# Moving weight splits, odd-key and rotated-query remainders and the token shift of a two-block decoder from ScalarE and VectorE to GpSimd

## The chip, the cores and the metric

One core of one Trainium2 chip runs the whole program. The metric is the device time of one execution in microseconds; the kernel before was timed in three runs. All profile times are from one profiled execution of it.

## What is computed

Two decoder blocks follow each other on 512 tokens of width 1024. The first has a gated unit, a sparse attention, cross-attention to a memory and a feed-forward part. The second has two layers, and the change is about these. In each layer one wide projection of the normed tokens (and of 256 context tokens) feeds three branches: a window attention "a", an attention "b" whose keys, values and queries are projected from small latents, and a gated convolution "c". The branches are gated and merged:

```python
def rms_norm_2(x, g):
    xf = x.astype(jnp.float32)
    y = xf * lax.rsqrt(jnp.mean(xf * xf, axis=-1, keepdims=True) + EPS)
    return (y * g.astype(jnp.float32)).astype(x.dtype)
...
    q = (rms_norm_2(q_lat, g_qa) @ w_qb).reshape(B, T, H_B, NOPE_B + ROPE_B)
    kv = (rms_norm_2(kv_lat, g_kva) @ w_kvb).reshape(B, T, H_B, NOPE_B + V_B)
...
    m = (jax.nn.sigmoid(ga) * ((ya * jax.nn.silu(za)) @ w_branch[0])
         + jax.nn.sigmoid(gb) * ((yb * jax.nn.silu(zb)) @ w_branch[1])
         + jax.nn.sigmoid(gc) * ((yc * jax.nn.silu(zc)) @ w_branch[2]))
    return m @ w_o
```

## The kernel before

Every operand of a matmul is held as a rounded high half and a remainder, the low half, and each product is three matmuls (`mm3`, lines 415 to 418: high by high, low by high, high by low). So all weights are **split** after they are loaded. The class `Stream` (lines 183 to 329) does it: SP loads chunks into tiles `raw`; `stat` (line 224) lets ScalarE sum squares for a scale; `total` (lines 425 to 433) turns the sums into the scale, by way of a VectorE sum, a matmul with ones, a VectorE step (L431), a power on GpSimd (L432) and a reciprocal on VectorE (L433); `pump` (line 237 on) writes the high half `wh` and, at the next call, `finish` (line 285 on) the low half `wl`. A ring of 9 pairs of `wh` and `wl` is filled ahead of use. Weights marked `fr` stay in 32 bits (high by ScalarE L266, low by VectorE L267); the others become 16-bit (high by ScalarE L273, or by GpSimd L271 where the block is marked `pool=True`; low by VectorE L291, in pieces of 512 columns).

The order of the work is written as Python generators: `tick` advances a clock of estimated costs, and calls the weight stream, the delayed chains (such as `norm_chain`) and the background attention. A scheduler then sets the order of each engine's queue by a priority that follows program order and by its own estimate of when each instruction is ready. Each engine takes its queue strictly in order.

In each layer, after the projections of branch a and the convolution, come the **latent stages**: latents kl and ql are projected and normed (`ev_kl`, `ev_ql`), and then `attention(b_items(...))` goes over 8 heads with 4 or 5 query tiles each. An item is: the S matmuls (L416 to L418, tile `S`, two buffers), the maximum on VectorE (L705), the exponential on ScalarE (L721, tile `P`), transposes on TensorE (L734), their high part on ScalarE (L738) and low part on VectorE (L739), and the output matmuls (L755). Between the items stand projections: `qb_head` makes the rotated queries of the next head (VectorE L1861, ScalarE L1862, VectorE L1863 for the latent tokens), `kb_pair` and `kb_odd` the keys (odd heads by way of a staging tile `kst`, split on ScalarE and VectorE at L421 and L422), `ev_vb` the values, and `agate` the gate of branch a with the weights `za`. The weights of the heads are split by `sp_` in `qb_blk` (3 or 4 moves each, ScalarE L1911 and VectorE L1912) and by the `fr` path for `kb_blk` and `vb_blk`. The merge's first gate and branch weights are read ahead while the attention still runs.

At a **layer boundary** `res_chain` (line 2179 on) adds the output to the tokens, and `norm_chain` (line 611 on) makes the next layer's normed tokens: squares on ScalarE (L614), `rstd` on GpSimd (six instructions, L404 to L412), gain on VectorE (L618), shift on VectorE (L620), then transposes on TensorE (L630). The boundaries lie near 815 to 845 us (first block to layer 0, four token tiles) and near 1705 to 1765 us (layer 0 to layer 1, six tiles, called 4, 5, 0, 1, 2, 3 in the order of their work). Two context tiles near 664 us take the same path.

## Time and profile before

| what | value |
|---|---|
| time, median of 3 runs (lowest, highest) | 2424.09 us (2421.36, 2431.43) |
| the profiled execution's own time | 2421.47 us |
| its span, first to last instruction | 2419.7 us |
| mean granted TensorE clock | 0.978 of full speed |
| attention b of layer 0 | about 1140 to 1340 us |
| attention b of layer 1 | about 2000 to 2140 us |

Times in rows are microseconds from the span's start unless marked ns. PE is TensorE, DVE VectorE, ACT ScalarE, POOL GpSimd. In a group's row the number behind the shape is the count, then busy time and mean ns of one, then the engine's idle time just before these instructions and what ended it. Square brackets in a timeline row hold the same idle time.

### The profile page before, as it was taken

Reading aid. Unit: us, or ns where it says so; the run is one execution under the profiler, and the core shown is the slowest. Engines: PE = TensorE matmul, PEld = TensorE weight load, DVE = VectorE, ACT = ScalarE, POOL = GpSimd, SP = SyncE. Lnnn points to the kernel's source line nnn. Section 1 sums busy time; section 2 is a strip of 40 time slices with the busy share of each in tenths; the row PEclk is TensorE's granted clock in tenths of the full one; section 3 lists DMA queues with packets and bytes.
Section 4 is the critical chain, followed back from the end, with each engine's and each line's share of the span. In section 5 each row is a group of like instructions: output and inputs, shape, how many; then the busy total and the mean of one; then the engine's idle time right before and its main releaser. Section 6 shows DMA issues by size and latency. Waiting matters only on the chain. (4 is left out here: it accounts for less than half of the span.)

```text
span 2419.7 us, 38066 instructions
## 1 busy us (share of the span) xinstructions
PE 2261.3 (93%) x14342; PEld 1505.2 (62%) x14342; DVE 1544.2 (64%) x3136; ACT 1298.1 (54%) x2745; POOL 320.7 (13%) x703
## 2 busy tenths in 40 slices
PE   7899899899999989999988999999779999899998
PEld 6777687544444557767767566557546567764446
DVE  6878678656665677665777444443777657865543
ACT  5656457746655455535777434323535457775532
POOL 4320321100100211004000000000621121000001
PEclk9899899899999999999999999999989999999999
DMA  4512445534443411112221422211421113233311
GB/s 158 140 47 71 141 144 199 172 101 153 155 140 106 122 50 38 46 40 65 79 74 56 137 79 61 79 42 63 156 86 50 42 38 108 71 115 113 103 44 61
DMA packets 182220, 226.67 MB, mean 94 GB/s; under 512 B 28556, under 2 KB 130876, under 8 KB 182036
## 3 DMA queue, kind: packets, MB, share of 16 engines
q1 hardware_dynamic: 158084, 187.67, 25.1%
q10 hardware_dynamic: 23952, 36.57, 4.4%
q8 instruction: 112, 1.84, 0.3%
q14 instruction: 72, 0.59, 0.1%
HBM read 207.33 MB, written 16.88 MB: 93 GB/s over the span
## 5 line engine op out<-in xcount | busy, mean ns | idle before, releaser
L416 PE MATMUL mm<-hTh,wh 128*128 128x512 f16 (+1 forms) x1040 | 392.6, 378 | 7.3 <-ACT wh L273 3.1
L291 DVE SCALAR_TENSOR_TENSOR wl<-raw,gs,wh 128x512 f16<-128x512 f32 (+2 forms) x420 | 296.6, 751 | 150.6 <-ACT wl L224 116.5
L417 PE MATMUL mm<-hTl,wh 128*128 128x512 f16 (+1 forms) x1040 | 392.4, 377 | 0.0
L418 PE MATMUL mm<-hTh,wl 128*128 128x512 f16 (+1 forms) x1040 | 391.2, 377 | 0.0
L224 ACT ACTIVATE wl<-raw 128x1024 f16<-128x1024 f32 (+3 forms) x242 | 222.9, 921 | 69.6 <-PE mm L417 37.3
L416 PEld LDWEIGHTS <-wh 128*128 128x128 f16 x1712 | 168.0, 98 | 147.4 <-issue 6.8
L417 PEld LDWEIGHTS <-wh 128*128 128x128 f16 x1712 | 168.0, 98 | 146.1 <-issue 9.6
L418 PEld LDWEIGHTS <-wl 128*128 128x128 f16 x1712 | 167.8, 98 | 143.9 <-issue 0.6
L738 ACT ACTIVATE ph<-mm 128x512 f16<-128x512 f32 (+2 forms) x300 | 146.1, 502 | 162.4 <-PE mm L734 156.1
L273 ACT ACTIVATE wh<-raw,gs 128x1024 f16<-128x1024 f32 x156 | 175.3, 1141 | 105.9 <-PE mm L417 83.0
L266 ACT ACTIVATE wh<-raw 128x512 fp32r<-128x512 f32 (+2 forms) x244 | 141.7, 613 | 142.2 <-PE mm L418 49.7
L739 DVE SCALAR_TENSOR_TENSOR pl<-mm,ph 128x512 f16<-128x512 f32 (+2 forms) x300 | 165.9, 567 | 73.6 <-ACT ph L738 71.1
L267 DVE TENSOR_TENSOR wl<-raw,wh 128x512 fp32r<-128x512 f32 (+2 forms) x244 | 156.1, 667 | 55.3 <-ACT wh L266 40.2
L432 POOL TENSOR_TENSOR gs<-gs,nh 128x1 f32<-128x1 f32 x66 | 40.6, 616 | 1125.2 <-DVE gs L431 1079.3
L416 PE MATMUL mm<-wh,hTh 128*128 128x512 f32 (+5 forms) x512 | 181.7, 356 | 5.5 <-DVE vf L1589 2.0
L418 PE MATMUL mm<-wh,hTl 128*128 128x512 f32 (+5 forms) x512 | 180.1, 352 | 1.8 <-DVE hTl L422 1.7
L417 PE MATMUL mm<-wl,hTh 128*128 128x512 f32 (+5 forms) x512 | 180.1, 352 | 0.3 <-DVE wl L267 0.3
L734 PE MATMUL mm<-ident,P 128*128 128x128 f32 x928 | 153.9, 283 | 5.9 <-ACT P L721 2.0
L721 ACT ACTIVATE P<-S,s 128x768 f32<-128x768 f32 (+4 forms) x160 | 105.8, 666 | 35.1 <-PE mm L734 18.0
L734 PEld LDWEIGHTS mm<-ident,P 128*128 128x128 f32 x928 | 108.6, 145 | 19.6 <-ACT P L721 2.9
L2133 DVE SCALAR_TENSOR_TENSOR z<-z,mm 128x256 f32<-128x256 f32 (+1 forms) x72 | 42.8, 596 | 107.2 <-PE mm L418 98.9
L271 POOL TENSOR_SCALAR wh<-raw,gs 128x1024 f16<-128x1024 f32 (+3 forms) x54 | 65.8, 1219 | 328.2 <-PE mm L417 209.9
(503 smaller groups left out, 5360.8 us busy)
## 6 DMA issues: line engine op xcount, KB each, us to landing
raw<-in_w_in_dram SPq DMA_DIRECT2D x124, 512.0 KB, 3.5
raw<-in_w_ff_dram SPq DMA_DIRECT2D x64, 512.0 KB, 4.5
raw<-in_w_mod_dram SPq DMA_DIRECT2D x48, 512.0 KB, 5.1
raw<-in_w_branch_dram SPq DMA_DIRECT2D x24, 512.0 KB, 3.4
raw<-in_w_o_dram SPq DMA_DIRECT2D x16, 512.0 KB, 4.0
raw<-in_cmp_w_dram SPq DMA_DIRECT2D x16, 256.0 KB, 3.5
raw<-in_w_out_dram SPq DMA_DIRECT2D x8, 512.0 KB, 3.6
raw<-in_w_mkv_dram SPq DMA_DIRECT2D x8, 512.0 KB, 3.7
```

The source lines that it names most:

```text
L224: nc.scalar.activation(lo[:, :b - a], t[:, a:b], AF.Square, accum_out=g.t[:, g.cols:g.cols + 1])
L266: nc.scalar.activation(hi[:, :m], src, AF.Copy)
L267: nc.vector.tensor_sub(lo[:, :m], src, hi[:, :m].bitcast(FT))
L273: nc.scalar.activation(hi[:, :m], src, AF.Copy, scale=s)
L291: self.nc.vector.scalar_tensor_tensor(l[:, b], src[:, b], s, h[:, b], op0=OP.mult, op1=OP.subtract)
L416: PE.matmul(ps, ah, bh, start=start, stop=False)
L417: PE.matmul(ps, ah, bl, start=False, stop=False)
L418: PE.matmul(ps, al, bh, start=False, stop=stop)
L721: ACT.activation(P, v[:, j, :], AF.Exp, bias=it.nb[:, j:j + 1], accum_out=it.den[:, j:j + 1])
L734: PE.transpose(ps[:, a - a0, :], it.P[0 if len(it.P) == 1 else j][:, c:c + 128], ident)
L738: ACT.activation(ph[:, :m], ps[:, :m], AF.Copy, scale=PSC)
L739: DVE.scalar_tensor_tensor(pl[:, :m], ps[:, :m], PSC, ph[:, :m], op0=OP.mult, op1=OP.subtract)
```

## The change

Six pieces of work go to GpSimd: both halves of the `fr` weights of `kb_blk` and `vb_blk`; all moves of the query weights in `sp_`; the low half of the queries of latent tokens; both halves of the odd keys; the token shift in `norm_chain`; and, for blocks marked `pool=2` (the four `za` blocks, and the gate and branch weights of the first merge step), the low half, now made by two instructions (the raw tile is scaled in place, then the high half is subtracted). The first merge step's high halves go from ScalarE to GpSimd with that mark. Lines below the first edit move by up to 8.

```diff
@@ -262,6 +262,9 @@
+        elif fr and u.blk.pool:
+            nc.gpsimd.tensor_copy(hi[:, :m], src)
+            nc.gpsimd.tensor_tensor(lo[:, :m], src, hi[:, :m].bitcast(FT), op=OP.subtract)
         elif fr:
@@ -286,9 +289,13 @@
-            for a in range(0, l.shape[-1], 512):
-                b = slice(a, min(a + 512, l.shape[-1]))
-                self.nc.vector.scalar_tensor_tensor(l[:, b], src[:, b], s, h[:, b], op0=OP.mult, op1=OP.subtract)
+            if u.blk.pool == 2:
+                self.nc.gpsimd.tensor_scalar(src, src, s, 1.0, op0=OP.mult, op1=OP.mult)
+                self.nc.gpsimd.tensor_tensor(l, src, h, op=OP.subtract)
+            else:
+                for a in range(0, l.shape[-1], 512):
...
@@ -617,7 +624,7 @@
-            DVE.tensor_add(xn, xn, S)
+            POOL.tensor_tensor(xn, xn, S, op=OP.add)
@@ -1860,7 +1867,7 @@
-                DVE.tensor_sub(lo[:, c0:c1], r, hi[:, c0:c1].bitcast(FT))
+                POOL.tensor_tensor(lo[:, c0:c1], r, hi[:, c0:c1].bitcast(FT), op=OP.subtract)
@@ -1892,7 +1899,8 @@
-        split(lay["kst"][64:128], kb[64:128, 2], kb[64:128, 3])
+        POOL.tensor_copy(kb[64:128, 2], lay["kst"][64:128])
+        POOL.tensor_tensor(kb[64:128, 3], lay["kst"][64:128], kb[64:128, 2].bitcast(FT), op=OP.subtract)
@@ -1908,8 +1916,8 @@
-                ACT.activation(hv[:, :, d:d + m], src[:, :, a:b], AF.Copy)
-                DVE.tensor_sub(lv[:, :, d:d + m], src[:, :, a:b], hv[:, :, d:d + m].bitcast(FT))
+                POOL.tensor_copy(hv[:, :, d:d + m], src[:, :, a:b])
+                POOL.tensor_tensor(lv[:, :, d:d + m], src[:, :, a:b], hv[:, :, d:d + m].bitcast(FT), op=OP.subtract)
...
-        return Blk([(dmas, [(0, [0, 1])])], 2, 128, fr=True)
+        return Blk([(dmas, [(0, [0, 1])])], 2, 128, fr=True, pool=True)
...
-        return Blk([(dmas, [(0, [0, 1])])], 2, 256, fr=True)
+        return Blk([(dmas, [(0, [0, 1])])], 2, 256, fr=True, pool=True)
...
-        za = [wblk(w[:, ZA + f * 128:ZA + (f + 1) * 128], pool=True) for f in range(4)]
+        za = [wblk(w[:, ZA + f * 128:ZA + (f + 1) * 128], pool=2) for f in range(4)]
...
-                    wblk(w[:, GA + b * 1024 + f2 * 256:GA + b * 1024 + (f2 + 1) * 256], g),
-                    wblk(A["w_branch_2"][i, b][:, f2 * 256:(f2 + 1) * 256], g))
+                    wblk(w[:, GA + b * 1024 + f2 * 256:GA + b * 1024 + (f2 + 1) * 256], g, pool=2 * (n + f2 == 0)),
+                    wblk(A["w_branch_2"][i, b][:, f2 * 256:(f2 + 1) * 256], g, pool=2 * (n + f2 == 0)))
```

Over both layers ScalarE loses 80 instructions, VectorE 130, and GpSimd gains 210. The scheduler puts the queues in a new order around them. In the attention b of layer 0 GpSimd's queue had only the powers of `total` (L432) and of `vscale` (L671), and the high half of one `za` unit (L271). Before, from the last `rstd` of the latents on:

```order
L671 TENSOR_TENSOR s_13125<-s_13079,nh 128x1
L432 TENSOR_TENSOR gs<-gs,nh 128x1 x2
L271 TENSOR_SCALAR wh<-raw,gs 128x1024
L671 TENSOR_TENSOR s_14084<-s_13982,nh 128x1
L432 TENSOR_TENSOR gs<-gs,nh 128x1 x3
```

Now, the stretch with the second of these powers (L432 is L439 here, L271 is L274, L671 is L678; `kst` is the staged odd keys, `y` the rotated queries):

```order
L1902 CAST kb<-kst 64x768
L439 TENSOR_TENSOR gs<-gs,nh 128x1
L1903 TENSOR_TENSOR kb<-kst,kb 64x768
L274 TENSOR_SCALAR wh<-raw,gs 128x1024
L293 TENSOR_SCALAR raw<-raw,gs 128x1024
L1870 TENSOR_TENSOR qb<-y,qb 128x512
L294 TENSOR_TENSOR wl<-raw,wh 128x1024
L274 TENSOR_SCALAR wh<-raw,gs 128x1024
L293 TENSOR_SCALAR raw<-raw,gs 128x1024
L294 TENSOR_TENSOR wl<-raw,wh 128x1024
L678 TENSOR_TENSOR s_14084<-s_13982,nh 128x1
```

The powers that VectorE waits for, and the query remainders, now stand behind wide splits on one queue.

The second place is GpSimd's queue at the boundary of layers 0 and 1 (`s2` are the scalars of `rstd`, `xn_18702` is the normed token tile 1, `gs` scales of weights). Before, from the residual's `rstd` of tile 3 to the first high halves of the layer's weights:

```order
L404 TENSOR_SCALAR s2_18788<-s2_18782 128x1
L406 TENSOR_TENSOR s2_18790<-s2_18788,nh_109 128x1
L408 TENSOR_TENSOR s2_18792<-s2_18790 128x1
L409 TENSOR_TENSOR s2_18792<-s2_18792,s2_18788 128x1
L432 TENSOR_TENSOR gs_18756<-gs_18756,nh_109 128x1
L410 TENSOR_SCALAR s2_18792<-s2_18792 128x1
L271 TENSOR_SCALAR wh_18899<-raw_154,gs_18756 128x1024
L271 TENSOR_SCALAR wh_18910<-raw_155,gs_18756 128x1024
L271 TENSOR_SCALAR wh_18933<-raw_153,gs_18756 128x1024
L412 TENSOR_TENSOR s2_18796<-s2_18790,s2_18792 128x1
```

And now:

```order
L411 TENSOR_SCALAR s2_18788<-s2_18782 128x1
L413 TENSOR_TENSOR s2_18790<-s2_18788,nh_109 128x1
L627 TENSOR_TENSOR xn_18702<-xn_18702,g_18569 128x1024
L439 TENSOR_TENSOR gs_18344<-gs_18344,nh_109 128x1
L415 TENSOR_TENSOR s2_18792<-s2_18790 128x1
L439 TENSOR_TENSOR gs_18756<-gs_18756,nh_109 128x1
L416 TENSOR_TENSOR s2_18792<-s2_18792,s2_18788 128x1
L274 TENSOR_SCALAR wh_18899<-raw_154,gs_18756 128x1024
L274 TENSOR_SCALAR wh_18910<-raw_155,gs_18756 128x1024
L274 TENSOR_SCALAR wh_18933<-raw_153,gs_18756 128x1024
L417 TENSOR_SCALAR s2_18792<-s2_18792 128x1
L419 TENSOR_TENSOR s2_18796<-s2_18790,s2_18792 128x1
```

The shift of tile 1 (L627) now stands inside the `rstd` of tile 3 and ahead of the weights' scale and high halves. Three more shifts (tiles 4, 5 and 0) stand ahead of these rows, and the last two behind them, next to each other.

## Rows read from the trace of the kernel before

**Rows 1.** The page, busy time by engine: us, share of the span, instructions.
```profile
PE 2261.3 (93%) x14342; PEld 1505.2 (62%) x14342; DVE 1544.2 (64%) x3136; ACT 1298.1 (54%) x2745; POOL 320.7 (13%) x703
```

**Rows 2.** Busy time in four stretches: window, its length, engines, granted clock, DMA share, GB/s.
```profile
1140.00:1340.00 200.00, 177.22 (x1341) 146.12 (x1339) 147.95 (x298) 140.90 (x338) 7.12 (x14) 0.97 0.26 80
2000.00:2140.00 140.00, 126.06 (x912) 101.87 (x911) 111.89 (x229) 107.12 (x246) 9.47 (x20) 0.98 0.29 86
815.00:845.00 30.00, 27.19 (x202) 19.64 (x200) 25.29 (x44) 15.17 (x38) 14.76 (x28) 1.00 0.54 171
1705.00:1765.00 60.00, 37.78 (x221) 30.57 (x220) 48.07 (x74) 31.21 (x64) 38.13 (x78) 0.86 0.51 167
```

**Rows 3.** Waits of TensorE, 1020 to 1360, then 1880 to 2180: total, times, longest.
```profile
PE S L416 <- ACT P L721: 12.1, 11, 2.5
...
PE S L416 <- ACT P L721: 6.9, 10, 1.1
PE S L1632 <- ACT P L721: 3.9, 5, 2.5
```

**Rows 4.** VectorE's groups by shape, 1075 to 1345, and the query-weight splits of both layers.
```profile
L291 DVE SCALAR_TENSOR_TENSOR wl<-raw,gs,wh 128x512 f16<-128x512 f32 x27 | 19.1, 747 | 9.3 <-ACT wl L224 6.1 <-POOL wh L271 3.2
...
L1863 DVE TENSOR_TENSOR qb<-y,qb 128x512 fp32r<-128x512 f32 x8 | 5.5, 684 | 1.7 <-ACT qb L1862 1.6
...
L422 DVE TENSOR_TENSOR kb<-kst,kb 64x768 fp32r<-64x768 f32 x3 | 2.9, 955 | 0.8 <-ACT kb L421 0.7
...
L267 DVE TENSOR_TENSOR wl<-raw,wh 128x256 fp32r<-128x256 f32 x4 | 1.7, 422 | 1.0 <-ACT wl L224 0.7 <-ACT wh L266 0.3
...
L267 DVE TENSOR_TENSOR wl<-raw,wh 128x512 fp32r<-128x512 f32 x2 | 1.4, 688 | 0.0
...
L1912 DVE TENSOR_TENSOR wl<-raw,wh x56: 191/202/459, 1109.2 to 2045.5; 128x48 fp32r<-128x48 f32 x32, 128x288 fp32r<-128x288 f32 x8, 128x192 fp32r<-128x192 f32 x8, 128x96 fp32r<-128x96 f32 x8
```

**Rows 5.** ScalarE: a group of 1075 to 1345; splits of both layers with min/median/max ns.
```profile
L273 ACT ACTIVATE wh<-raw,gs 128x1024 f16<-128x1024 f32 x9 | 10.3, 1149 | 10.0 <-PE mm L417 10.0
...
L1911 ACT ACTIVATE wh<-raw x56: 225/232/445, 1108.7 to 2041.5; 128x48 fp32r<-128x48 f32 x32, 128x288 fp32r<-128x288 f32 x8, 128x192 fp32r<-128x192 f32 x8, 128x96 fp32r<-128x96 f32 x8
...
L421 ACT ACTIVATE kb<-kst x6: 842/843/847, 1202.9 to 2127.1; 64x768 fp32r<-64x768 f32 x6
```

**Rows 6.** The chain that ended last, moved instructions in both attentions: start, us, what.
```profile
1236.13 1.39 DVE wl L291 x2
1238.52 0.60 DVE qb L1863
...
2041.23 0.53 ACT wh L1911 x3
...
2075.72 1.32 DVE wl L291 x2
```

**Rows 7.** GpSimd's widest group, whole span, by shape.
```profile
L271 POOL TENSOR_SCALAR wh<-raw,gs 128x1024 f16<-128x1024 f32 x40 | 53.0, 1328 | 222.0 <-PE mm L417 127.6 <-PE mm L418 69.1 <-issue 24.4
```

**Rows 8.** Timeline near 823 us, GpSimd's high halves, then VectorE's low halves.
```profile
815.78 1.13 POOL L271 TENSOR_SCALAR wh<-raw,gs 128x1024 f16<-128x1024 f32 x1
...
821.29 2.06 POOL L271 TENSOR_SCALAR wh<-raw,gs 128x1024 f16<-128x1024 f32 x1
...
823.38 2.27 DVE L291 SCALAR_TENSOR_TENSOR wl<-raw,gs,wh 128x512 f16<-128x512 f32 x2 [1.02 <-POOL wh L271]
...
826.25 1.40 DVE L291 SCALAR_TENSOR_TENSOR wl<-raw,gs,wh 128x512 f16<-128x512 f32 x2
```

**Rows 9.** VectorE's reciprocal behind GpSimd's power, 1075 to 1345.
```profile
L433 DVE RECIPROCAL gs<-gs 128x1 f32<-128x1 f32 x7 | 1.1, 160 | 1.9 <-POOL gs L432 1.8
```

**Rows 10.** The token shift on VectorE, all twelve: min/median/max ns.
```profile
L620 DVE TENSOR_TENSOR xn<-xn,g x12: 1209/1215/1226, 664.3 to 1759.5; 128x1024 f32<-128x1024 f32 x12
```

**Rows 11.** Timeline of GpSimd at the boundary of layers 0 and 1.
```profile
1727.85 0.83 POOL L2193 TENSOR_TENSOR s<-s,oms 128x1 f32<-128x1 f32 x1 [3.00 <-ACT y L2189]
...
1734.55 0.22 POOL L404 TENSOR_SCALAR s<-s 128x1 f32<-128x1 f32 x1 [3.82 <-ACT xn L614]
...
1741.59 4.67 POOL L271 TENSOR_SCALAR wh<-raw,gs 128x1024 f16<-128x1024 f32 x3
```

**Rows 12.** Timeline of TensorE at the same boundary, its two longest waits.
```profile
1750.80 0.69 PE L1581 MATMUL S<-ident,kd 128*128 128x128 f32 x2 [8.64 <-ACT kd L1556]
...
1757.22 1.94 PE L630 MATMUL S<-ident,xn 128*128 128x128 f32 x8 [5.74 <-DVE hTl L422]
```

More of the change, by code (lines that the diff above doesn't have):

```diff
@@ L288, in finish @@
             self.half = None
-            for a in range(0, l.shape[-1], 512):
-                b = slice(a, min(a + 512, l.shape[-1]))
-                self.nc.vector.scalar_tensor_tensor(l[:, b], src[:, b], s, h[:, b], op0=OP.mult, op1=OP.subtract)
+            if u.blk.pool == 2:
[3 more added lines that the diff above has]
+                for a in range(0, l.shape[-1], 512):
+                    b = slice(a, min(a + 512, l.shape[-1]))
+                    self.nc.vector.scalar_tensor_tensor(l[:, b], src[:, b], s, h[:, b], op0=OP.mult, op1=OP.subtract)
             u.ready = True
```

## The prediction

> **What bounds the kernel now.** I read the page first, then busy time by stretch, TensorE's waits, the chain that ended last, and the timelines where the change puts something. The page shows TensorE busy for 2261 of 2420 us and GpSimd for 321 us [rows 1]. So a gain can only come from time in which TensorE idles, and from clock lost after idling. Busy time by stretch shows where that is [rows 2]. In the attention of layer 0 TensorE idles 200 - 177.2 = 22.8 us, in that of layer 1 140 - 126.1 = 13.9 us, while VectorE and ScalarE are busy for 70 to 80% and GpSimd for 4 to 7%. The boundary of layers 0 and 1 idles 60 - 37.8 = 22.2 us, with VectorE at 48 and GpSimd at 38 of 60 us. The granted clock is 0.97, 0.98 and 0.86 there, just under the upper level of 2.4 GHz. If each stretch had run at 1.00, the attentions would have saved at most 0.03 x 177 + 0.02 x 126 = 7.8 us.
>
> TensorE's waits say what ends the idling: in the attentions mostly "S matmul behind the exponential", 12.1 us in layer 0 and 6.9 + 3.9 us in layer 1 [rows 3]. An exponential is late because ScalarE, or VectorE with the maximum ahead of it, is still at something else in its queue. The chain that ended last runs through these queues, and some of the instructions that move lie on it [rows 6].
>
> **What the change takes off.** Per layer, in and just before the attention, VectorE loses: 14 pieces of low halves (four `za` units and three units of the first merge step, two pieces each) x 0.747 = 10.5 us; 8 query remainders x 0.684 = 5.5; 3 odd-key remainders x 0.955 = 2.9; 4 x 0.422 + 2 x 0.688 = 3.1 for key and value weights; and 28 query-weight pieces, 16 of 48 columns at 0.2 and 12 wider ones between 0.2 and 0.46, taken at 0.35, 7.4 [rows 4]. That is 29 us. ScalarE loses 3 x 1.149 = 3.4, 28 pieces by the same rule 7.8, 3 x 0.843 = 2.5, and about 3 for key and value weights, as long as their VectorE partners [rows 4, 5]: 17 us.
>
> Little of it sits on the path. In the covered parts of the two attentions (1225 to 1340 and 2000 to 2140 us) I find nine such pieces on the chain, of 0.35 to 1.41 us, 7.4 us in all; four of them are shown [rows 6]. For all 340 us that is 7.4 x 340 / 255 = 9.9 us. The bounds of the gain are 0 (another instruction of the same queue is late instead) and 36.7 us of idling plus 7.8 us of clock, 44 us. I take 16: the 10 us on the chain, because that is the nearest row, plus a third of the clock, 2.6, plus 3 for idling that shrinks because queues with a seventh less in them catch up sooner.
>
> **What it adds on GpSimd.** One input: 1024 columns take 1.13 us undisturbed [rows 8], 1.33 on average [rows 7], so 1.1 ns a column. Two inputs of that width do not occur. They cost at least one pass (1.13 us), at most two disturbed ones (2 x 2.06 = 4.1) [rows 8]; I take two undisturbed passes, 2.3 us. The Trainium skill (GPSIMD Engine Reference, section 3.1) gives 4497 ns for 2048 columns; by that it would be 2.25 us, and no run here shows it yet. Per layer the two-input work is 7 low halves of 1024, 8 remainders of 512, 3 of 768, weight pieces of 2048 and 3072 in sum: 18.7 thousand columns x 2.25 ns = 42 us. The one-input work (7 scalings and 3 high halves of 1024, the other high halves 7.4 thousand) is 17.7 x 1.1 = 19 us. With some 0.15 us for each of about 100 instructions that makes 75 us per layer, beside 7 to 10 us now. GpSimd then stands at a third in the attention: not a bound, and the consumers are far off: a query remainder or an odd key is made four items (some 18 us) ahead of its use, weight halves up to nine units ahead. I cost lateness at nothing; without that slack each L1870 behind a wide low half would cost up to 2.3 us, once per head.
>
> Two things are charged. VectorE's reciprocal waits for GpSimd's power seven times per layer, 1.8 us in all [rows 9]. The power now stands behind splits; what waits behind the reciprocal is VectorE's whole queue, the maxima among it. Half of the powers meet a busy GpSimd for half a wide instruction, with one or two VectorE instructions between as cover: +1 us.
>
> The other is contention. Beside a high half on GpSimd, two low halves took 2.27 us instead of 1.40, and GpSimd's 2.06 instead of 1.13 [rows 8]. There VectorE's instruction reads two tensors from SBUF and GpSimd's reads one. The Trainium skill (SBUF — State Buffer, section "Who interferes with whom") says that a VectorE instruction with two SBUF inputs contends with a GpSimd instruction that reads SBUF, and that the second to issue blocks fully; the trace's 0.87 us fits. In the rows themselves: 10 low halves per layer and some 26 other two-input instructions remain; a third of them meets a GpSimd instruction and waits some 0.9 us, 36 x 0.34 x 0.9 = 11 us per layer, mostly in VectorE's own slack. A seventh of it on the path is +3 us for both layers. The bounds are 0 and 22.
>
> **The boundaries.** The token shift takes VectorE 1.215 us [rows 10]; on GpSimd it is 2.3. At the boundary of layers 0 and 1 GpSimd's queue has the `rstd` chains back to back. In its timeline the idle gaps that could take a shift are 3.00 and 3.82 us [rows 11]. Four shifts, 9.2 us, now stand ahead of the three high halves that start at 1741.59, so those come 9.2 - 6.8 = 2.4 us later at best and 9.2 at worst. The last two shifts stand one behind the other, 2 x (2.3 - 1.2) = 2.2 us longer. VectorE gains 7.3 us, but as it waits for GpSimd's scalars, that helps only in part. TensorE already waits 8.64 and 5.74 us here [rows 12], so nothing hides a delay. Bounds -3 and +11; I take +6. At the first boundary, with four tiles, TensorE idles 2.8 us of 30 and GpSimd is half free [rows 2]: +1, between -2 and +4. The two context tiles sit beside the feed-forward matmuls: nothing.
>
> **The sum**: -16 + 1 + 3 + 7 = -5 us on the profiled execution's 2421.5 is 2416.5. The median of the runs before lies 2.6 us above that execution, so I predict **2419 us**. A measurement of this kernel can tell some 0.5%, 12 us, from no change.
>
> **Rivals.**
> *A, faster: the queues relax.* Relief off the chain counts as well: with 29 + 17 us gone per layer, half or more of the idling and of the lost clock vanishes, 24 us, the boundary costs 2, contention 1: 2403 us. For it: almost every long wait in the attention ends on a late exponential [rows 3]. Against it: only 7.4 us of moved work lies on the chain, and the sums of squares, which also do, stay on ScalarE.
> *B, slower: the shared read port.* VectorE is the engine that must not stop, and each GpSimd instruction of 2.3 us can hold a two-input VectorE instruction, with the maxima queued behind it. It decides once the mean wait exceeds some 1.2 us and half of the waits fall on the path: 72 x 0.34 x 1.2 x 0.5 = 15 us; with all of them on the path 29. With the gain cut to 6 and the boundary at +11 that gives 2421.5 - 6 + 22 + 11 + 2.6 = 2451, or 2439 with the boundary as forecast and half the waits. For it: the pair at 823 us. Against it: maxima and P's low halves read PSUM, so they need no second SBUF read. By the rule of the Trainium skill cited above (SBUF — State Buffer, section "Who interferes with whom") every such meeting would block in full.
> *C, the forecast*: both effects are small and nearly cancel.
>
> **Chances.** C 0.40, with a range of its own of 2412 to 2434; A 0.36; B 0.24. Faster by over 0.5% (under 2412) is A, 0.36; within 0.5% is C, 0.40; slower (over 2436) is B, 0.24. A reaches down to 2421.5 - 44 + 2.6 = 2380 with all of the idling gone, of which I leave out the last part; B up to 2451. The range that leaves out a tenth on either side is 2394 to 2442.
>
> **What would show it.** TensorE's idle time in the two attentions falls from 36.7 to about 25 us; VectorE is busy there for some 10% less, GpSimd for a third. At the boundary of layers 0 and 1 the idling grows from 22 to about 28 us, and shifts of 2.3 us or more (over 2.5 where they meet VectorE) lie in GpSimd's row. A is right if the waits for the exponential fall under 10 us in sum; B, if the remaining low halves on VectorE take over 0.95 us on average instead of 0.747. I am wrong in the working if the two-input instruction of 1024 columns takes under 1.5 or over 3 us, or if TensorE comes to wait for a GpSimd result directly.

## The result and the profile after

The changed kernel is slower by 1%: 2448.96 us in the median of four runs (2445.43 to 2454.35), against 2424.79 us before. The ratio is 1.0098, with an interval of 1.0070 to 1.0127. The forecast was 2419 us, with a range up to 2442: the time lies outside it, on rival B's side; slower by over 0.5% had a chance of 0.24. The profiled execution took 2448.86 us, its span is 2446.9 us and its mean granted clock 0.969.

The line of busy times on the page of the changed kernel, to be read against [rows 1]:

```profile
PE 2276.5 (93%) x14342; PEld 1515.5 (62%) x14342; DVE 1498.5 (61%) x3006; ACT 1271.9 (52%) x2665; POOL 479.7 (20%) x913
```

GpSimd has 159 us of work more (the prices of the prediction gave 2 x 75 + 12 x 2.3 = 178). VectorE lost 46 us and ScalarE 26. TensorE is busy for 15 us longer with the same matmuls, at a mean granted clock of 0.969 instead of 0.978; where these 15 us lie is said below the table of stages.

Busy time by stretch, in the windows that hold the same work as [rows 2]: the context tiles, the first boundary, layer 0's attention, the boundary of the layers and layer 1's attention (columns as there; the windows are shifted and longer by what the kernel has fallen behind):

```profile
651.00:696.00 45.00, 38.25 (x167) 16.69 (x166) 29.87 (x50) 24.49 (x39) 9.74 (x12) 0.92 0.58 192
821.00:856.00 35.00, 30.08 (x206) 20.66 (x204) 21.66 (x40) 15.43 (x38) 23.30 (x32) 0.95 0.45 147
1150.00:1350.00 200.00, 180.45 (x1345) 149.65 (x1344) 138.65 (x263) 132.80 (x316) 64.52 (x99) 0.95 0.27 84
1714.00:1782.00 68.00, 42.87 (x225) 33.59 (x224) 42.50 (x68) 31.53 (x64) 47.70 (x85) 0.77 0.44 147
2016.00:2168.00 152.00, 130.87 (x922) 106.54 (x921) 101.73 (x192) 99.30 (x226) 67.45 (x101) 0.93 0.27 81
```

VectorE is less busy in both attentions (148 to 139 us, 112 to 102), and yet TensorE idles 19.5 and 21.1 us instead of 22.8 and 13.9, at a lower clock. Of these, 4.6 and 8.5 us are waits for the latents, which are still normed at the start of both windows; without them the idling would be 14.9 and 12.6 us. TensorE's longest waits over the whole span, in order of their sum, before:

```profile
PE S L416 <- ACT P L721: 21.4, 23, 2.5
...
PE S L630 <- DVE xn L618: 12.5, 3, 10.9
```

And in the changed kernel:

```profile
PE S L637 <- DVE xn L625: 24.8, 6, 10.6
PE S L423 <- ACT P L728: 12.6, 12, 2.5
...
PE mm L423 <- DVE oc L1247: 6.8, 3, 3.8
...
PE mm L437 <- DVE sb L435: 6.0, 3, 2.6
PE S L637 <- POOL xn L627: 5.6, 1, 5.6
PE mm L423 <- DVE z L2199: 5.4, 2, 5.0
```

The waits for the exponential, the largest before, have shrunk. At the top stands now the wait for a normed tile `xn` of VectorE, twice what it was (its longest, 10.6 us, was there before; the added ones are the latents'), and there is one for a shift on GpSimd (L627).

To see where the time went, I paired each instruction of TensorE with its like in the trace of before (same line, tiles and shape) and took how far it starts behind, which can be read to some 0.3 us. This lag is 0.9 us at 645 us, where nothing has changed yet, and 27.7 at the end. It grows in few places (times of before, us; the other columns are the kernels of the experiments below, one profiled execution each):

| stage | changed | E1 | E2 | E3 | E4 | E5 | E6 | E7 | E8 | E9 | E10 |
|---|---|---|---|---|---|---|---|---|---|---|---|
| context tiles, 645 to 700 | +5.1 | 0.0 | +5.4 | +0.9 | +0.1 | -0.5 | -0.6 | -0.6 | +1.4 | -0.3 | +0.8 |
| first boundary, 800 to 865 | +4.5 | 0.0 | +4.5 | 0.0 | 0.0 | 0.0 | 0.0 | 0.0 | +7.0 | 0.0 | 0.0 |
| latent norms, layer 0, 1085 to 1150 | +7.6 | +7.8 | 0.0 | 0.0 | +8.1 | +2.4 | 0.0 | 0.0 | 0.0 | 0.0 | 0.0 |
| attention, layer 0, to 1400 | -8.9 | -10.1 | +2.8 | -9.8 | +0.9 | -9.5 | -4.9 | +1.6 | -1.1 | -6.7 | -16.5 |
| boundary of layers, 1690 to 1800 | +7.5 | +1.2 | +7.0 | +1.1 | +0.6 | +1.6 | +2.2 | +0.7 | +9.5 | +1.8 | +1.2 |
| latent norms, layer 1, 1970 to 2045 | +9.8 | +9.8 | 0.0 | -0.3 | +10.1 | +3.6 | -1.9 | -0.1 | 0.0 | -0.4 | -0.3 |
| attention, layer 1, to 2250 | +1.6 | +2.1 | -1.6 | +0.8 | -0.2 | +0.4 | -2.5 | +4.5 | +0.5 | -0.5 | -5.5 |

What is left out (start to 645, and 865 to 1085) is unchanged code; there single executions lie up to 6 us apart, so a column's sum is not the kernel's time; the medians are. So the loss is 17 us at the three places of the token shift, 17 us at the latent norms, and the relief is 9 us in layer 0's attention and none in layer 1's.

Of the 35 us that these five stages lose, some 20 are longer idling of TensorE; the other 15 are its longer busy time with the same matmuls, behind the waits, where the granted clock is lower (1.00 before and 0.94 now, 1.00 and 0.98, 1.00 and 0.95, 0.92 and 0.87, 0.98 and 0.92, for the five from the top of the table). Where the clock stayed at 1.00 (700 to 800 us, 1400 to 1690 us) the busy time is the same. Levels of the clock are 1.00 (2.4 GHz) and 0.50 (1.2 GHz); other figures are means of a stretch.

**The latent norms.** The timeline of GpSimd in the changed kernel, while one query latent tile is normed. Its `rstd` is six instructions on `s` (L411 to L419), each waiting for the one before:

```profile
1140.55 0.22 POOL L411 TENSOR_SCALAR s<-s 128x1 f32<-128x1 f32 x1 [2.56 <-ACT xn L621]
1140.86 0.57 POOL L413 TENSOR_TENSOR s<-s,nh 128x1 f32<-128x1 f32 x1
1141.42 1.12 POOL L274 TENSOR_SCALAR wh<-raw,gs 128x1024 f16<-128x1024 f32 x1
1142.51 0.19 POOL L415 TENSOR_TENSOR s<-s 128x1 f32<-128x1 f32 x1
...
1147.37 2.13 POOL L294 TENSOR_TENSOR wl<-raw,wh 128x1024 f16<-128x1024 f32 x1
1149.46 0.19 POOL L417 TENSOR_SCALAR s<-s 128x1 f32<-128x1 f32 x1
1149.62 2.13 POOL L294 TENSOR_TENSOR wl<-raw,wh 128x1024 f16<-128x1024 f32 x1
1151.70 1.26 POOL L267 TENSOR_TENSOR wl<-raw,wh 128x512 fp32r<-128x512 f32 x1
1152.92 1.28 POOL L1920 TENSOR_TENSOR wl<-raw,wh 128x288 fp32r<-128x288 f32 x3
1154.16 0.19 POOL L419 TENSOR_TENSOR s<-s,s 128x1 f32<-128x1 f32 x1
```

The chain takes 13.8 us, from 1140.55 to 1154.35, since the splits of the gate block, the value block and the first query weights stand between its steps. In the kernel before such a chain took 2.2 us:

```profile
1142.54 0.22 POOL L404 TENSOR_SCALAR s<-s 128x1 f32<-128x1 f32 x1 [2.64 <-ACT xn L614]
...
1144.56 0.19 POOL L412 TENSOR_TENSOR s<-s,s 128x1 f32<-128x1 f32 x1
```

Behind it VectorE idles for 9.11 us, with the evacuations that stand behind the gain in its queue, and TensorE for 3.04; in layer 1 TensorE idles 6.70 us behind one such tile. With a second, shorter wait in each layer that is 4.6 and 8.5 us; TensorE's longer busy time, at the lower clock, adds 3.2 us in layer 0 and 2.8 in layer 1. Changed kernel, VectorE's and then TensorE's instruction there:

```profile
1154.38 0.71 DVE L625 SCALAR_TENSOR_TENSOR xn<-z,s,g 128x384 f32<-128x384 f32 x1 [9.11 <-POOL s L419]
```

```profile
1155.15 0.55 PE L637 MATMUL S<-ident,xn 128*128 128x128 f32 x3 [3.04 <-DVE xn L625]
...
2026.25 0.87 PE L637 MATMUL S<-ident,xn 128*128 128x128 f32 x3 [6.70 <-DVE xn L625]
```

**The context tiles.** Timeline of the changed kernel near 674 us, GpSimd, VectorE, TensorE:

```profile
673.68 2.73 POOL L627 TENSOR_TENSOR xn<-xn,g 128x1024 f32<-128x1024 f32 x1 [1.46 <-DVE xn L625]
```

```profile
673.46 3.50 DVE L298 SCALAR_TENSOR_TENSOR wl<-raw,gs,wh 128x512 f16<-128x512 f32 x2
676.88 0.74 DVE L1247 SCALAR_TENSOR_TENSOR oc<-mm,gs,oc 128x512 f32<-128x512 f32 x1
```

```profile
677.67 0.58 PE L423 MATMUL mm<-hTh,wh 128*128 128x512 f16 x1 [3.77 <-DVE oc L1247]
678.05 0.63 PE L424 MATMUL mm<-hTl,wh 128*128 128x512 f16 x1
```

Nobody waits for this shift. But two low halves on VectorE take 3.50 us beside it (1.40 alone, [rows 8]), the evacuation `oc` behind them is late, TensorE idles 3.77 us instead of 0.53, and the matmuls after that take 0.6 us instead of 0.38, until the clock is back: it is at its lower level, 0.50, from 677.6 to 680.0 us, and the granted clock of the stretch is 0.92, where it was 1.00 before. Not all of the delay is the meeting: before, this evacuation came straight behind the gain, and the new order puts the pair of low halves ahead of it, 1.4 us by itself; the meeting adds 2.1.

**The boundary of the layers.** TensorE waited 8.64 and 5.74 us [rows 12]. Now its longest waits are three:

```profile
1742.93 0.37 PE L423 MATMUL mm<-wh,hc 128*128 128x256 f16 x1 [5.00 <-DVE z L2199]
...
1767.66 0.69 PE L1588 MATMUL S<-ident,kd 128*128 128x128 f32 x2 [11.34 <-ACT kd L1563]
...
1774.00 1.97 PE L637 MATMUL S<-ident,xn 128*128 128x128 f32 x8 [5.65 <-POOL xn L627]
```

The second has grown by 2.7 us and the first is new, while shorter waits have gone. The third is not new: before, the same matmul waited 5.74 us for an evacuation. In all, TensorE idles 25.1 us in the stretch instead of 22.2; the larger part of the loss is that it is busy for 42.9 us instead of 37.8 (with four matmuls more in the window, 0.6 us), as the granted clock falls from 0.86 to 0.77.

### The profile page after: what moved, and what is told of

The parts are those of the page before. It is cut to its first block, busy times and chain, and to the rows that moved or that the text cites. A ratio compares the mean times of both kernels' runs of the same rounds, so it can differ in the third digit from the quotient of the medians.

```text
span 2446.9 us, 38147 instructions
## 1 busy us (share of the span) xinstructions
PE 2276.5 (93%) x14342; PEld 1515.5 (62%) x14342; DVE 1498.5 (61%) x3006; ACT 1271.9 (52%) x2665; POOL 479.7 (20%) x913
## 3 DMA queue, kind: packets, MB, share of 16 engines
q8 instruction: 112, 1.84, 0.3%
## 4 chain that ended last, share of the span: by engine, by line
PE 74%; DVE 7%; ACT 6%; issue 5%; DMA 4%; POOL 4%; ACTq 0%; SPq 0%; DVEq 0%; POOLq 0%
PE mm L423 20%; PE mm L424 20%; PE mm L425 20%; PE mm L741 3%; PE O L762 2%; DVE wl L298 2%; DMA raw<-in_w_in_dram 1%; ACT wl L224 1%; ACT P L728 1%; DVE pl L746 1%; PE S L423 1%; DMA raw<-in_w_mod_dram 1%; POOL s L413 1%; ACT ph L745 1%; PE S L424 1%
## 5 line engine op out<-in xcount | busy, mean ns | idle before, releaser
L298 DVE SCALAR_TENSOR_TENSOR wl<-raw,gs,wh 128x512 f16<-128x512 f32 (+2 forms) x392 | 283.8, 769 | 148.8 <-ACT wl L224 117.2
L276 ACT ACTIVATE wh<-raw,gs 128x1024 f16<-128x1024 f32 x150 | 168.5, 1141 | 116.5 <-PE mm L424 82.4
L439 POOL TENSOR_TENSOR gs<-gs,nh 128x1 f32<-128x1 f32 x66 | 39.3, 596 | 867.2 <-DVE gs L438 830.8
L269 ACT ACTIVATE wh<-raw 128x512 fp32r<-128x512 f32 (+1 forms) x232 | 135.9, 620 | 135.1 <-PE mm L425 48.0
L270 DVE TENSOR_TENSOR wl<-raw,wh 128x512 fp32r<-128x512 f32 (+1 forms) x232 | 150.1, 676 | 54.5 <-ACT wh L269 40.5
L274 POOL TENSOR_SCALAR wh<-raw,gs 128x1024 f16<-128x1024 f32 (+3 forms) x60 | 70.3, 1173 | 331.4 <-PE mm L424 216.3
L712 DVE TENSOR_REDUCE s<-S 128x1 f32<-128x768 f32 (+4 forms) x112 | 97.3, 874 | 22.2 <-PE S L425 15.9
```

What stands on the lines that cost most here:

```text
L269: nc.scalar.activation(hi[:, :m], src, AF.Copy)
L270: nc.vector.tensor_sub(lo[:, :m], src, hi[:, :m].bitcast(FT))
L276: nc.scalar.activation(hi[:, :m], src, AF.Copy, scale=s)
L298: self.nc.vector.scalar_tensor_tensor(l[:, b], src[:, b], s, h[:, b], op0=OP.mult, op1=OP.subtract)
```

## The experiments

Two theories were set against each other. **Q**: GpSimd has one queue, and short chains or single results that TensorE waits for now stand behind, or are, long instructions. **P**: rival B of the prediction, GpSimd's reads slow VectorE wherever they meet. E1 to E4 are the first set of the texts quoted below.

### E1 to E4: the shift and the early splits, undone and alone

E1 is the changed kernel with the shift back:

```diff
-            POOL.tensor_tensor(xn, xn, S, op=OP.add)
+            DVE.tensor_add(xn, xn, S)
```

> The changed kernel with the token shift back on VectorE, all else as changed. Theory Q (GpSimd's one queue): the time is lost where a short chain that TensorE waits for stands behind long work on GpSimd. Matched matmul for matmul, the changed kernel falls behind by 5 us at the context tiles (650 to 700 us), 4.5 at the first boundary and 7.6 at the boundary of the layers, all three places of the shift: so about 17 us come back, 2449 - 17 = 2432 us. Rival P (read port): GpSimd's added 159 us slow VectorE wherever both read SBUF, in proportion to their length; twelve shifts of 2.46 us are 30 us of the 159, a fifth of some 43 us of loss (27 net, 16 of relief): 8 us come back, 2441 us.

Measured: 2435.24 us, 1.0032 (1.0020 to 1.0045) of before. E2 is the opposite, the kernel before with that line alone changed.

> The kernel before with the token shift alone on GpSimd. Theory Q: the same three places lose 5, 4.5 and 7.6 us with no relief elsewhere, 2424 + 17 = 2441 us. Rival P: 2424 + 8 = 2432 us, and the loss appears as longer VectorE instructions, not as waits for the shift.

Measured: 2439.10 us, 1.0056 (1.0039 to 1.0073). The shift costs 14 us either way, at its own three places, which lose 0.0, 0.0 and 1.2 us in E1 and as much as ever in E2 (5.4, 4.5 and 7.0). In E2 the context tiles lose 5.4 us by way of a VectorE instruction, as P has it; at the second boundary TensorE waits for a shift itself, 9.9 us at the longest.

E3 is E1 with the early blocks split as before:

```diff
...
+                if h < 3:
+                    ACT.activation(hv[:, :, d:d + m], src[:, :, a:b], AF.Copy)
+                    DVE.tensor_sub(lv[:, :, d:d + m], src[:, :, a:b], hv[:, :, d:d + m].bitcast(FT))
+                else:
...
-        return Blk([(dmas, [(0, [0, 1])])], 2, 128, fr=True, pool=True)
+        return Blk([(dmas, [(0, [0, 1])])], 2, 128, fr=True, pool=p > 1)
...
-        return Blk([(dmas, [(0, [0, 1])])], 2, 256, fr=True, pool=True)
+        return Blk([(dmas, [(0, [0, 1])])], 2, 256, fr=True, pool=g > 1)
...
-        za = [wblk(w[:, ZA + f * 128:ZA + (f + 1) * 128], pool=2) for f in range(4)]
+        za = [wblk(w[:, ZA + f * 128:ZA + (f + 1) * 128], pool=2 if f > 2 else True) for f in range(4)]
```

> As the first kernel of this set (shift on VectorE), and also the weight blocks that are split ahead of the attention (gate blocks 0 to 2, both value blocks, the first two key blocks, query weights of heads 0 to 2) split as before, so that no wide split stands among GpSimd's rstd chains of the latent norms. The later splits, the query remainders and the odd keys stay on GpSimd. Theory Q: the 7 us of layer 0 and 12 of layer 1 that are lost at the latent norms go too, part of the relief of the first heads is given up: 2432 - 18 + 2 = 2416 us, under the kernel before. Rival P: these blocks are some 40 of GpSimd's 159 us and give back 11: 2430 us.

Measured: 2416.72 us, 0.9959 (0.9943 to 0.9975): faster than the kernel before. E4 is the kernel before with those blocks alone on GpSimd:

```diff
...
-        return Blk([(dmas, [(0, [0, 1])])], 2, 128, fr=True)
+        return Blk([(dmas, [(0, [0, 1])])], 2, 128, fr=True, pool=p < 2)
...
-        za = [wblk(w[:, ZA + f * 128:ZA + (f + 1) * 128], pool=True) for f in range(4)]
+        za = [wblk(w[:, ZA + f * 128:ZA + (f + 1) * 128], pool=2 if f < 3 else True) for f in range(4)]
```

> The kernel before with only those early weight blocks moved to GpSimd (gate blocks 0 to 2, both value blocks, key blocks 0 and 1, query weights of heads 0 to 2). Theory Q: GpSimd's rstd chains of the latent norms stand behind them in both layers, TensorE waits for the normed query latents: 2424 + 18 less a little relief = 2440 us. Rival P: 2424 + 11, less the same relief, = 2432 us, with no single long wait for the normed latents.

Measured: 2443.06 us, 1.0069 (1.0051 to 1.0088). All four times lie within 3.3 us of what Q gave and, but for E1, 7 us or more from P; E1 lies between (Q 2432, P 2441). The latent norms lose 8 and 10 us in the changed kernel, E1 and E4, which have the early splits and the chains on GpSimd, and nothing in the kernels that have the early splits elsewhere. VectorE's group of norm gains for the query latents of layer 0 (384 wide) tells the same; in E1, then in E3 (the third number is the idle time before them):

```profile
L625 DVE SCALAR_TENSOR_TENSOR xn<-z,s,g 128x384 f32<-128x384 f32 x6 | 3.8, 632 | 14.1 <-POOL s L419 14.1
```

```profile
L625 DVE SCALAR_TENSOR_TENSOR xn<-z,s,g 128x384 f32<-128x384 f32 x6 | 3.7, 616 | 2.7 <-POOL s L419 2.6
```

### E5: the chain taken off the queue, the splits left on it

E1 with the latents' six small instructions on VectorE:

```diff
-    def rstd(ms, n, p=128):
+    def rstd(ms, n, p=128, vec=False):
+        E = DVE if vec else POOL
...
-        POOL.tensor_tensor(y, a, neghalf[:p, :n], op=OP.pow)
+        if vec:
+            DVE.reciprocal(y, a)
+        else:
+            POOL.tensor_tensor(y, a, neghalf[:p, :n], op=OP.pow)
...
-        r = rstd(ss, 1)
+        r = rstd(ss, 1, vec=w < 512)
```

The other four of the six go by `E` too. This kernel leaves out the root: a reciprocal stands in the power's place, so its latents are scaled otherwise, and only its time is of use.

> The changed kernel with the token shift back on VectorE (2435 us) and, with all weight splits left on GpSimd, the six small instructions behind each latent norm's sum of squares moved from GpSimd to VectorE (with a reciprocal in the power's place, so the latents are scaled otherwise than in the reference). Theory Q: nothing that TensorE waits for then stands behind the early splits; the 8 us lost at layer 0's latent norms and 9 at layer 1's come back: 2435 - 17 = 2418 us. Rival P (the splits cost by slowing VectorE): the splits are all still there and VectorE has 60 small instructions per layer more: 2435 to 2440 us.

Measured: 2423.74 us, 0.9986 (0.9972 to 1.0000), 11.5 us under E1 and nearer to Q (2418) than to P (2435 to 2440). GpSimd does all the work of E1's splits at the same places; only the chain no longer passes through it. The latent norms lose 2.4 and 3.6 us instead of 7.8 and 9.8. So two thirds of the loss are the queue, not the splits' presence. What is left fits P: a gain of layer 0 takes 0.92 us instead of 0.63, and steps of the chain, now on VectorE, are held by the same splits. Group of the gains, then a step of the chain on VectorE that takes 0.16 us elsewhere, then GpSimd's split beside it:

```profile
L629 DVE SCALAR_TENSOR_TENSOR xn<-z,s,g 128x384 f32<-128x384 f32 x6 | 5.5, 923 | 0.2
```

```profile
1143.26 1.84 DVE L423 TENSOR_TENSOR s<-s,s 128x1 f32<-128x1 f32 x1
```

```profile
1142.96 2.12 POOL L294 TENSOR_TENSOR wl<-raw,wh 128x1024 f16<-128x1024 f32 x1
```

What the holds cost TensorE here was not separated.

### E6 and E7: the query remainders

Layer 1's attention gained nothing in the changed kernel. There TensorE waits twice, 2.59 us each, for a sum of squares that VectorE should make. Changed kernel, timeline at the first of them, GpSimd, VectorE, TensorE:

```profile
2120.55 1.53 POOL L1870 TENSOR_TENSOR qb<-y,qb 128x512 fp32r<-128x512 f32 x1 [3.25 <-ACT qb L1869]
```

```profile
2120.21 2.42 DVE L298 SCALAR_TENSOR_TENSOR wl<-raw,gs,wh 128x512 f16<-128x512 f32 x2
2122.55 0.14 DVE L435 TENSOR_REDUCE sb<-gs 128x1 bf16<-128x3 f32 x1
```

```profile
2122.75 0.16 PE L437 MATMUL mm<-sb,onesb 128*128 128x1 bf16 x1 [2.59 <-DVE sb L435]
```

The pair of low halves takes 2.42 us instead of 1.40 beside the query remainder on GpSimd, and the ones matmul of `total` stands ahead of other matmuls on TensorE. E6 is E3 with the remainder on VectorE again:

```diff
-                POOL.tensor_tensor(lo[:, c0:c1], r, hi[:, c0:c1].bitcast(FT), op=OP.subtract)
+                DVE.tensor_sub(lo[:, c0:c1], r, hi[:, c0:c1].bitcast(FT))
```

> The third kernel of the first set (2417 us) with the query remainders back on VectorE. In layer 1's attention two low halves on VectorE took 1.76 us instead of 0.75 beside a query remainder on GpSimd, and a sum behind each made TensorE wait 2.6 us. Theory Q: the port matters only at such single meetings; without the remainders these two waits shrink by 1 us each, but VectorE has 16 x 0.68 = 11 us more, of which a third or so lies on the path: 2417 - 2 + 4 = 2419 us. Rival P: the meetings are what eats layer 1's gain, both waits of 2.6 us go with the clock lost behind them: 2411 us.

Measured: 2414.62 us, 0.9961 (0.9948 to 0.9975), no different from E3, and between the two theories (Q 2419, P 2411). Layer 1's attention gains 2.5 us instead of losing 0.8, layer 0's gains 4.9 instead of 9.8. The two waits are still there, 1.6 us at most instead of 2.6: the meeting made 1.0 us of each, the order of the queues the rest. E7 is the kernel before with that line the other way round, and with the odd keys' two halves as in the change.

> The kernel before with only the query remainders and the odd keys' two halves on GpSimd. They take 2 x (8 x 0.68 + 3 x 0.96) = 17 us from VectorE and 7 from ScalarE, about a fourth of what the whole change takes. Theory Q: no chain that TensorE waits for passes GpSimd here but the scales' powers; a fourth to a half of the relief of the attention of layer 0 (10 us in the kernels with the shift back): 2424 - 4 = 2420 us. Rival P: low halves on VectorE meet the remainders in both layers, some five meetings of 1.0 us in the path: 2424 - 4 + 5 = 2425 us or more.

Measured: 2433.83 us, 1.0031 (1.0019 to 1.0044), slower than before, where Q gave 2420 and P 2425 or more. Alone, the moved pieces lose in both attentions (+1.6 and +4.5; the profiled execution is one of the shorter, 2428.17 us). VectorE's low halves in layer 1's attention, in E7, average 958 ns instead of 746 before:

```profile
L291 DVE SCALAR_TENSOR_TENSOR wl<-raw,gs,wh 128x512 f16<-128x512 f32 x19 | 17.5, 958 | 1.2 <-ACT wl L224 1.2
```

Seven of the low halves in both attentions took 1.75 to 1.78 us, each beside one of the 16 remainders (an eighth, 1.18 us, beside a high half). So the remainders' move takes 16 x 0.684 = 10.9 us from VectorE (the odd keys' 5.7 come on top) and gives 7 x 1.0 back, two of them, at 2100 and 2137 us, ahead of sums for which TensorE then waits 2.58 and 2.60 us; the kernel before has no such wait in this attention. P is the better theory here. But E6 has the same two waits at 1.6 us without a meeting, so the new order of the queues has its part; where the rest of the 8 us arises was not traced.

### E8: the shift in four pieces

E2 with four instructions for each shift (the edit is against the kernel before):

```diff
-            DVE.tensor_add(xn, xn, S)
+            for a in range(0, 1024, 256):
+                POOL.tensor_tensor(xn[:, a:a + 256], xn[:, a:a + 256], S[:, a:a + 256], op=OP.add)
```

> The kernel before with the token shift on GpSimd as in the second kernel of the first set (2439 us), but in four pieces of 256 columns. There, at 674 us, a low half on VectorE took 2.83 us instead of 0.75 beside a shift, and TensorE waited 4 us behind it. Rival P, at this place: a piece of some 0.73 us can hold a VectorE instruction for no longer than that, so the low half takes 1.5 us at most and the loss at the context tiles falls from 5 to about 1.5 us; with four pieces 0.6 us longer than one instruction, some six of them in the path: 2439 - 3.5 + 3.5 = 2439 us, or 2436 if the boundaries gain too. Theory Q without any port: the loss at the context tiles stays at 5 us or grows, 2443 us.

Measured: 2443.30 us, 1.0074 (1.0055 to 1.0093): no gain, since the boundaries lose 7.0 and 9.5 us. But at the context tiles the loss falls from 5.4 to 1.4 us, as P had it (1.5; Q without a port 5 or more). GpSimd and VectorE there, in E8:

```profile
673.73 4.05 POOL L621 TENSOR_TENSOR xn<-xn,g 128x256 f32<-128x256 f32 x4 [1.46 <-DVE xn L618]
```

```profile
673.51 1.88 DVE L291 SCALAR_TENSOR_TENSOR wl<-raw,gs,wh 128x512 f16<-128x512 f32 x2
```

The pair takes 1.88 us instead of 3.50 beside more GpSimd time than before, and two later low halves are held for 0.5 us each: what holds VectorE there for 2.1 us is the one long instruction, which it must wait out.

### E9 and E10: two attempts at a better kernel

E9 was meant to be E3 with the query remainders on GpSimd in layer 0 alone:

```diff
-                POOL.tensor_tensor(lo[:, c0:c1], r, hi[:, c0:c1].bitcast(FT), op=OP.subtract)
+                if 1 in segs:
+                    POOL.tensor_tensor(lo[:, c0:c1], r, hi[:, c0:c1].bitcast(FT), op=OP.subtract)
+                else:
+                    DVE.tensor_sub(lo[:, c0:c1], r, hi[:, c0:c1].bitcast(FT))
```

> The third kernel of the first set (early weight blocks and shift back, 2417 us) with the query remainders on GpSimd in layer 0 only, on VectorE in layer 1. Theory: a query remainder on GpSimd takes 0.68 us from VectorE and gives 1.0 us back where it meets a low half there; in layer 0 the third kernel gained 10 us in the attention, with the remainders on VectorE 5; in layer 1 it gained nothing, with the remainders on VectorE 4.4. Taken together, 10 + 4.4 less some 1 us elsewhere: 2425 - 13 = 2412 us. Rival (the scheduler's order, not the place of the remainders, makes the differences of 5 us): no better than either, 2415 to 2417 us.

Measured: 2417.99 us, 0.9960 (0.9946 to 0.9975). The edit did less than was meant. For all heads but the first, `qb_head` is called with one segment at a time, so that `1 in segs` is false where the remainder is made: one remainder of 16 runs on GpSimd, 15 on VectorE.

```profile
L1871 POOL TENSOR_TENSOR qb<-y,qb x1: 1429/1429/1429, 1161.4 to 1161.4; 128x512 fp32r<-128x512 f32 x1
```

```profile
L1873 DVE TENSOR_TENSOR qb<-y,qb x15: 678/692/2386, 1166.7 to 2132.9; 128x512 fp32r<-128x512 f32 x15
```

So E9 is E6 but for one instruction, and whether the gains of E3 and E6 add up stays untested. It shows something else: with one instruction moved, the attentions' columns of E6 and E9 differ by 2 us (-4.9 and -6.7, -2.5 and -0.5), so a difference of that size between two executions says nothing by itself. E10 is E3 with the whole first merge step split on GpSimd:

```diff
-                    wblk(w[:, GA + b * 1024 + f2 * 256:GA + b * 1024 + (f2 + 1) * 256], g, pool=2 * (n + f2 == 0)),
-                    wblk(A["w_branch_2"][i, b][:, f2 * 256:(f2 + 1) * 256], g, pool=2 * (n + f2 == 0)))
+                    wblk(w[:, GA + b * 1024 + f2 * 256:GA + b * 1024 + (f2 + 1) * 256], g, pool=2 * (n == 0)),
+                    wblk(A["w_branch_2"][i, b][:, f2 * 256:(f2 + 1) * 256], g, pool=2 * (n == 0)))
```

> The third kernel of the first set (2417 us) with all four pairs of blocks of the first merge step split on GpSimd, high and low half, not only the first pair. The low halves that meet the query remainders in the attentions then stand on the same engine as the remainders and can't hold VectorE; GpSimd has some 20 blocks of 3.3 us more. Theory (meetings on the port cost layer 1 its gain): the meetings of 1.0 us and the waits of 2.6 us for the scale's sum go, layer 1 gains 4 us: 2412 us. Rival (GpSimd's one queue again): the powers of the scales and the query remainders stand behind 3.3 us of split per block, TensorE waits for the next head's queries or a scale: 2417 to 2425 us.

Measured: 2404.90 us, 0.9909 (0.9895 to 0.9923), the fastest of all, 12 us under E3 and 7 under what the theory gave. Layer 0's attention gains 16.5 us, layer 1's 5.5. TensorE's waits of E10 in layer 1's attention and just before it:

```profile
PE mm L741 <- DVE pl L746: 3.7, 5, 1.8
...
PE S L423 <- ACT P L728: 1.2, 3, 0.5
```

The waits for the sum are gone, and those for the exponential are 1.2 us against 6.9 before [rows 3]. In the two attentions VectorE has no low half left to meet a remainder, where E3 has 20 (E10 1140 to 1340 and 1988 to 2122 us, E3 1140 to 1335 and 1995 to 2136). E10 takes the meetings away and more work off VectorE and ScalarE at once; which of the two gave more was not separated.

## Why the prediction was wrong

By its own steps:

- **Prices: right.** A low half of 1024 columns on GpSimd took 2.13 to 2.16 us, a shift 2.35 us in the median, against 2.3 forecast. By the Trainium skill (GPSIMD Engine Reference, section 3.1) it would be 2.25 us, an estimate; the trace agrees. GpSimd is busy for 0.32 and 0.44 of the attentions, a third forecast. One reading was off: the high half of 2.06 us in [rows 8] had ended, at 823.35 us, before the pair of low halves began. The one beside that pair took 1.64 us; the 2.06 arose beside a token shift on VectorE, so GpSimd can be the one that waits. The 0.87 us of VectorE's wait stands.
- **"I cost lateness at nothing": the step that failed.** It looked at the consumers of what moved (remainders, odd keys, weight halves) and at the scales' powers, and found slack. What already stood on GpSimd's queue and was now pushed back was not counted: the `rstd` chains of the latent norms, six instructions per tile, right where the first weight blocks are split. The trace of the kernel before had them (near 1142 us, shown above); the prediction listed `rstd` for the boundaries only. It measured +7.6 and +9.8 us, 17 of the 27 us net, where the sum had nothing. E3, E4 and E5 show the cause from three sides.
- **The clock: counted as a gain only.** The sum had a third of the clock coming back, 2.6 us, and no clock lost behind new waits. The five stages that lose time lost 15 us by it.
- **"The two context tiles ...: nothing": wrong**, +5.1 us. No consumer is near, but the port is: a shift holds a low half that now stands ahead of an evacuation. E8 shows that the length of the one instruction sets the hold.
- **The boundaries: under-sized.** Forecast +6 and +1, measured +7.5 and +4.5; the first lies in its bounds, the second just over its +4. At the boundary of the layers the idling was to grow from 22 to about 28 us; it grew to 25.1, and the rest of the loss is busy time at the lower clock.
- **The relief: -16 forecast, -7 measured**, all of it in layer 0 (-8.9, and +1.6 in layer 1). TensorE's idling in the two attentions was to fall from 36.7 to about 25 us; it is 40.7, or 27.6 without the 13.1 us of waits for the latents. Waits for the exponential fell to 6.3 us in layer 0 and 2.5 + 3.6 in layer 1, from the 12.1 and 6.9 + 3.9 of [rows 3]; rival A's sign, under 10 us in sum, was not reached. But waits for the normed tiles and for two sums took their place. With the early splits back and more low halves moved the relief is 22 us (E10), so the sign and the size were possible, the place was not.
- **Contention: the sum over-sized, the place missed.** 11 us of VectorE's waiting per layer were forecast. VectorE's instructions that lasted over 0.2 us more than the median of their line and shape are 20 before, with 13.5 us of excess, and 35 after, with 24.4: 11 us more in all, meetings with shifts included. Of these 11 us, 2.1 at the context tiles and 1.0 each at two sums lay in TensorE's path.
- **The reciprocals (+1)**: VectorE waited for GpSimd's power 1.0 us in layer 0's stretch, 1.8 before [rows 9]. No loss.

**The rivals.** B had the sign and, by chance, the size (2451), but its mechanism explains only a part: the context tiles and the two meetings in layer 1, some 7 us with the clock. Its sign in the trace, low halves over 0.95 us on average, is just missed in layer 0 and met in layer 1. Changed kernel, VectorE's groups in the two attentions (1150 to 1350, 2016 to 2168):

```profile
L298 DVE SCALAR_TENSOR_TENSOR wl<-raw,gs,wh 128x512 f16<-128x512 f32 x10 | 9.1, 946 | 0.4 <-ACT wl L224 0.4
...
L298 DVE SCALAR_TENSOR_TENSOR wl<-raw,gs,wh 128x512 f16<-128x512 f32 x10 | 10.1, 1050 | 0.7 <-ACT wl L224 0.7
```

So it was a poor test: it sees the meetings and not what they cost. The Trainium skill's rule that was cited with it (SBUF — State Buffer, section "Who interferes with whom") agrees with the trace at these meetings: a low half, two inputs from SBUF, took 2.83 us instead of 0.75 beside a shift, and 1.76 beside a remainder. It does not at 664 us, shown at the end, where the shift was the one that waited though it began before the second VectorE instruction. That TensorE would come to wait for a GpSimd result directly was named as a sign that the working is wrong; it did, 5.65 us at L637, though that matmul had waited as long before.

## What to carry to other kernels

Before work is put on an idle engine, list what already stands on its queue and how many steps of it a critical chain takes there: 20% busy was no slack for a chain of six 0.2 to 0.6 us steps that had 2 us instructions put between them. Move what is needed late, in stretches where no such chain runs, and leave the rest (E3: 2417 us; E10: 2405). Price a new wait with the clock lost behind it: here 20 us of idling cost 15 us more. Where two engines slow each other when both read SBUF, look at what the moved piece will meet: the remainders and odd keys alone (E7) took some 17 us from VectorE and made the kernel 8 us slower, and E10, in which nothing was left for the remainders to meet, was the fastest. That the meetings made this difference is not shown: E10 also took more work off VectorE, and E3 and E6, with and without the remainders moved, were equal.

## What the runs showed of the hardware

- In the following meetings a VectorE instruction with two inputs from SBUF waited for nearly all that was left of GpSimd's, some 0.2 us less. At the context tiles the second low half began at 674.12 us, 2.29 us of the shift were left, and it took 2.08 us longer than 0.75; at 2120 us 1.21 us of the remainder were left, and the low half took 1.01 us longer; in E2 a norm gain began 0.08 us behind a shift, 2.26 us were left, and it took 3.34 us instead of 1.28. GpSimd's instruction and VectorE's, in E2:

```profile
1776.13 2.34 POOL L620 TENSOR_TENSOR xn<-xn,g 128x1024 f32<-128x1024 f32 x1
```

```profile
1776.21 3.34 DVE L618 SCALAR_TENSOR_TENSOR xn<-xt,s,g 128x1024 f32<-128x1024 f32 x1 [0.48 <-POOL s L412]
```

- Not every meeting does so. At the other context tile of the changed kernel two VectorE instructions with two such inputs took no longer than alone (0.68 us each; the second began at 664.84 us, after the shift), and the shift took 3.27 us instead of 2.35. An evacuation with one input from PSUM, beside the same shift, took its usual 0.74 us. GpSimd, then VectorE:

```profile
664.46 3.27 POOL L627 TENSOR_TENSOR xn<-xn,g 128x1024 f32<-128x1024 f32 x1 [12.97 <-DVE oc L1247]
```

```profile
664.24 1.28 DVE L1402 TENSOR_TENSOR ffl<-z,ffh 128x512 f16<-128x512 f32 x2
```

- In these rows GpSimd's time goes by columns, not by elements: the odd key's remainder on 64 partitions and 768 columns took 1.84 us, 2.4 ns a column, as the shift on 128 partitions did (2.35 us for 1024, 2.3 ns).
- A wait costs TensorE more than its length: at the context tiles the wait grew by 3.2 us (3.77 for 0.53) and the lag by 5.1, since the matmuls behind it ran at the lower clock (0.50 for a part of it).
